# Branch products of two branches moved ahead of the gates in a one-core fp32 attention and feed-forward block

## The chip, the cores and the metric

The kernel runs on one core of a Trainium2 chip. The metric is device time in microseconds (us) of one execution; the median of three runs of the kernel before is 1457.66 us (1457.46 to 1459.04). A core has TensorE (PE: matmuls, and PEld for its weight loads), VectorE (DVE), ScalarE (ACT), GpSimd (POOL) and SyncE (SP, which here issues most of the DMAs). Each engine works through its own queue in order, and they wait for one another by semaphores.

## The reference, cut to what matters

One layer for 256 tokens of width 2048, all in fp32. The part that the change touches:

```python
h = rms_norm(x, g_mix[l]); proj = h @ w_in[l]
fq, fk, fv, f_logit, sq, sk, sv, mq, gates = jnp.split(proj, cuts, axis=-1)
o_fox = ...   # forgetting attention, 6 heads
o_sb  = ...   # stick-breaking attention, 6 heads
o_mem = ...   # attention to 256 memory tokens, 4 heads
g = jax.nn.sigmoid(gates.reshape(b, s, N_BRANCH, D_MODEL) + b_gate[l])
merged = (g[:, :, 0] * (o_fox @ w_br_fox[l])
          + g[:, :, 1] * (o_sb @ w_br_sb[l])
          + g[:, :, 2] * (o_mem @ w_br_mem[l]))
x = x + merged @ w_out[l]
```

Then a gated feed-forward part with a short causal convolution follows.

## The kernel before, in words

**Arithmetic.** Every fp32 weight piece (128 partitions x 1024 columns, `raw`) is split into a high part `hi` by a ScalarE copy and a low part `lo` by a VectorE subtraction (`piece`, L137 to L148, for plain products; `parts`, L374 to L380, in blocks). The pools hold four buffers each of `raw`, `hi` and `lo`. A product is then three matmuls (`three`, L382 to L386): high times high, low times high (both with `hi`), and high times `lo`; the third, L386, is the first that needs `lo`. The activations (`xT`, `oT`, `mT`) are the stationary side, 128 x 128; the weights stream with 512 columns.

**Plain products.** `product` (L158 to L173) runs over the k-tiles two at a time: one 512 KB load, one split, twelve matmuls into two PSUM banks (two row halves t), then one `tick`. `proj` is `product` with `xT` and `w_in`.

**Blocks.** `blocked` (L423 to L541) computes 1024 columns for all 16 k-tiles, in eight pairs of k-tiles, by a plan of letters. An "e" pair takes eight 2x2 block products, 24 matmuls. An "s" pair takes seven products after Strassen, 21 matmuls, from sums of weights and sums of activations. For gates the weight sums are formed on VectorE in `prepared` (L492 to L500, four 512-column additions), which is called at the end of the "e" pair before; the activation sums `xs` come from `x_sums` (L1041). The results X of the direct products hold four PSUM banks, the shared products Y four more, from the first "s" pair on. Just before that pair `ready` runs the queue of pending work dry and loads the gate's two bias tiles. After the last "s" pair `gathered` (L1104) adds the Ys up on VectorE, in steps beside the last two "e" pairs; after the block `scaled_sums` (L1132) adds X times the row scale, and a sigmoid on ScalarE finishes the gate (L1149 to L1151).

**Order.** Work that shall run beside matmuls is a generator, given to `later`. Each `tick` (L104) advances the generators that are active (at most `window` of them, two or three) by a step; a number yielded is a count of ticks to skip. `background` generators are advanced by ticks of plain products and of all blocks but the gates'. Two of them matter: `x_sums`, and `half_sums` (L264), which forms sums of weights of later stages: load, sums, store, with a period in ticks. `ready` and `finish` run ticks until nothing is pending. Instructions go to the engines' queues by a list scheduler that works from program order and its own estimate of when operands are there; those given to `in_order` keep their program order among themselves, and in the gate stage all matmuls of `three` do (`ordered`, L1093).

**The stage.** The six stick-breaking heads (`sb_head`, L988) are queued three at a time. Heads 3 to 5 end in the plain gate block that follows. For each half m of the 2048 columns the three gates come first (branch order 0 forget, 1 stick-breaking, 2 memory), then for two pieces n of 512 columns the three branch products (order: forget, memory, stick-breaking; L1154 to L1168), multiplied with the gates straight from PSUM and added up on VectorE; `merged_T` transposes the sum, and the product with `w_out` follows. By `g_plans` (L228) the first gate of the first half has the plan "", that is plain products of 16 k-tiles for each of its two pieces (L1138 to L1144); the other five have "esesesee", three "s" pairs out of eight. The sigmoids of the plain gate are queued by `sigmoids` (L1088) when the second gate's block reaches its first "s" pair. All these tiles (gates, sums of gate weights, heads) are of one pool of 14 buffers, 128 x 1024 (`block`).

Of the kernel before, what the change touches and what calls it, by code (L numbers as in the profile page):

```python
# [10 lines left out]
F32 = mybir.dt.float32  # L11
F32R = mybir.dt.float32r
AF = mybir.ActivationFunctionType
ALU = mybir.AluOpType
AX = mybir.AxisListType

P = 128
S = 256
NT = S // P
# [24 lines left out]
def hybrid_block(  # L44
# [25 lines left out]
    nc = tc.nc  # L70
# [26 lines left out]
    waiting, active, window = deque(), [], [2]  # L97

    def later(gen):
        waiting.append(gen)  # L100
# [18 lines left out]
    issued = set()  # L119
# [105 lines left out]


    o_plans = ("eessssse", "eessssse")
    g_plans = (("", "esesesee", "esesesee"), ("esesesee", "esesesee", "esesesee"))  # L228
    d_plans = (
        "efefefef" + "sef" * 4 + "ssefsfssfssee",  # L230
        "efsss" * 3 + "efssfsssssee",
# [4 lines left out]
    in_order = tc.keep_in_program_order  # L236
# [428 lines left out]
    gp = mix.enter_context(tc.tile_pool(name="gp", bufs=3))  # L665

    def block(name, dt=F32):
        return bp.tile([P, 1024], dt, tag="blk", name=name)
# [4 lines left out]
    def rows_of(b):  # L673
        return b.rearrange("p (t n) -> p t n", t=NT)
# [68 lines left out]
    w = {}  # L743
# [295 lines left out]
    xs = cst.tile([P, GS, 4, 2, P], F32R, tag="xres", name="xs")  # L1039

    def x_sums():  # L1041
        for _ in range(4):
            yield
        for p in range(GS):
            pair_sums(xT.pair(p), (junk(f"xa_{p}"), junk(f"xr_{p}")), [(xs[:, p], slice(0, 4))])
            for _ in range(3):
                yield

    background.append(x_sums())
    background.append(  # L1050
        half_sums(lambda name: gp.tile([P, 1024], F32, tag="pre", bufs=1, name=name), 8, 2, 5, "merged")
    )


# [30 lines left out]

    raw_g = lambda name: wp.tile([P, PIECE], F32, tag="raw", name=name)

    def sigmoids(tiles):  # L1088
        for v in tiles:
            in_order(nc.scalar.activation(v, v, AF.Sigmoid))  # L1090
            yield

    ordered[0] = True  # L1093
    for m in range(2):
        gate = []
        for b, plan in enumerate(g_plans[m]):
            g, bias = [], []

            def biases(m=m, b=b, bias=bias):
                for n in (2 * m, 2 * m + 1):  # L1100
                    bias.append(gp.tile([P, 512], F32, tag="bg", name=f"bg_{n}_{b}"))
                    nc.sync.dma_start(bias[-1], b_gate[0, b, n * 512 : (n + 1) * 512].partition_broadcast(P))

            def gathered(n0, Y, m=m, b=b, g=g, bias=bias):  # L1104

                w = block(f"gw_{m}_{b}")
                g += [rows_of(block(f"g_{m}_{b}_{n}")) for n in range(2)]
                e, f = w[:, :512], w[:, 512:]
                scaled = lambda dst, src, c, n: nc.vector.scalar_tensor_tensor(
                    dst, src, c, bias[n], ALU.mult, ALU.add  # L1110
                )
                nc.scalar.copy(e, Y[0])
                scaled(g[0][:, 0], Y[0], rstd[:, 0:1], 0)
                nc.vector.tensor_tensor(e, e, Y[1], ALU.add)
                yield
                nc.vector.tensor_tensor(f, e, Y[2], ALU.add)
                scaled(g[1][:, 0], f, rneg[:, 0:1], 1)
                nc.vector.tensor_tensor(f, e, Y[3], ALU.add)
                scaled(g[0][:, 1], f, rstd[:, 1:2], 0)
                yield  # L1120
                nc.vector.tensor_tensor(f, f, Y[2], ALU.add)
                scaled(g[1][:, 1], f, rneg[:, 1:2], 1)

            def ready():
                finish()
                if "heads" not in issued:
                    issued.add("heads")
                    window[0] = 2
                    later(sigmoids(gate[0] + gate[1]))
                biases()  # L1130

            def scaled_sums(n, ps, add):  # L1132
                for t in range(NT):
                    nc.vector.scalar_tensor_tensor(g[n][:, t], ps[t], rstd[:, t : t + 1], add[t], ALU.mult, ALU.add)

            c0 = C_GATE + b * D + m * PIECE
            gate.append(g)
            if not plan:  # L1138
                biases()
                for n in range(2):  # L1140
                    ps = proj(c0 + n * 512, 512, f"g{n}_{b}")
                    g.append(rows_of(block(f"g_{m}_{b}_{n}")))
                    scaled_sums(n, ps, [bias[n]] * NT)
                continue  # L1144
            X = blocked(
                "g", w_in, f"{m}{b}", c0, plan, lambda p, j: xT(2 * p + j), lambda p, f: xs[:, p, f], raw_g, block,
                gathered, ready,
            )
            for n in range(2):  # L1149
                scaled_sums(n, [X[t][n] for t in range(NT)], [g[n][:, t] for t in range(NT)])  # L1150
                nc.scalar.activation(g[n], g[n], AF.Sigmoid)  # L1151
        if m == 1:
            later(merged_sums())
        for n in range(2):  # L1154
            acc = gate[branches[0][3]][n]
            for i, (w, k0, nk, b) in enumerate(branches):
                ps = product(lambda k: oT[:, k0 + k], w[0], nk, (2 * m + n) * 512, 512, f"b{2 * m + n}_{b}")
                if (m, n, i) == (1, 0, 1):
                    xres = cst.tile([P, NT, D], F32, tag="xres", name="xres_again")
# [270 lines left out]
```

## Time and profile before

| | before |
|---|---|
| median of 3 runs | 1457.66 us |
| the profiled execution | 1457.28 us |
| its span, first to last instruction | 1455.6 us |
| granted TensorE clock | 1.000 |
| HBM read, written | 353.24 MB, 43.00 MB |

The rows of the profile name a line of the kernel (L386), an engine, an operation and its tiles, output<-inputs, with buffer numbers left out. In rows in order of time the first number is the start in us from the span's beginning, the second the length, and a bracket at the end tells how long the engine stood idle before the row and what released it. Matmul rows overlap: the time from one start to the next is what a matmul costs in a dense stream. The names: `raw_g`, `hi_g`, `lo_g` are weight pieces of a gate, `t_g`, `hi_t_g`, `lo_t_g` the sums of them, `xg` and `yg` the banks X and Y, `g` the gate tiles (and the banks of the plain gate), `gw` the scratch tile of `gathered`, `b` the banks of branch products, `z` and `sb` the bank and tile of a stick-breaking head, `fx` and `fa` those of a forget head, `pre_d` and `kept_d` the sums for a later stage.

### The profile page before, as it was taken

The numbers are of one execution on the slowest core, as the hardware profiler recorded it, in microseconds if no ns is written. First come the engines' busy times: TensorE is split into PE (matmuls) and PEld (weight loads), VectorE is DVE, ScalarE is ACT, GpSimd is POOL, SyncE is SP. The second block draws the span as 40 slices with busy tenths as digits, with TensorE's granted clock in tenths as the row PEclk, the third lists the DMA queues.
The fourth block names the chain that finished last, engine by engine and source line by source line (L and its number), as shares of the span: only waits on it lengthen the run. The fifth ranks groups of instructions, "written<-read, shape, count | busy, mean of one in ns | idle before, by whom it ended". The sixth has DMA issues, their size and how long they took to land.

```text
span 1455.6 us, 20647 instructions
## 1 busy us (share of the span) xinstructions
PE 1449.9 (100%) x7289; PEld 1226.9 (84%) x7289; DVE 1228.8 (84%) x1824; ACT 857.0 (59%) x1222; POOL 32.7 (2%) x70
## 2 busy tenths in 40 slices
PE   9999999999999999999999999999999999999998
PEld 7888888888888888888888888888888888888887
DVE  5788778776898899998887888888888877999988
ACT  6755445464564556546676656556556556676775
POOL 0000011010000000000000000000000011000000
PEclk9999999999999999999999999999999999999999
DMA  8797899777668576788877888888888899889996
GB/s 293 228 349 249 320 334 324 266 254 217 210 204 269 180 226 201 268 263 266 300 216 240 287 271 300 280 272 301 280 284 295 271 257 253 260 283 344 322 340 231
DMA packets 169414, 393.41 MB, mean 270 GB/s; under 512 B 12906, under 2 KB 30206, under 8 KB 165086
## 3 DMA queue, kind: packets, MB, share of 16 engines
q1 hardware_dynamic: 165822, 384.87, 79.5%
q0 software_dynamic: 2160, 5.12, 1.9%
q10 hardware_dynamic: 1328, 2.11, 0.4%
q8 instruction: 57, 0.93, 0.2%
q14 instruction: 47, 0.39, 0.1%
HBM read 353.24 MB, written 43.00 MB: 272 GB/s over the span
## 4 chain that ended last, share of the span: by engine, by line
PE 99%; DMA 0%; SPq 0%; DVE 0%; ACT 0%; issue 0%; DVEq 0%
PE u L1318 22%; PE u L1319 11%; PE xg L384 4%; PE xg L386 4%; PE xg L385 4%; PE xd L386 3%; PE xd L385 3%; PE xd L384 3%; PE s L386 2%; PE s L384 2%; PE f L384 2%; PE f L386 2%; PE f L385 2%; PE s L385 2%; PE b L386 2%; PE b L384 2%
## 5 line engine op out<-in xcount | busy, mean ns | idle before, releaser
L1318 PE MATMUL u<-hT,hi_u 128*128 128x512 f32 x1232 | 428.4, 394 | 0.0
L1319 PE MATMUL u<-hT,lo_u 128*128 128x256 f32 x1232 | 341.3, 277 | 0.0
L1318 PEld LDWEIGHTS u<-hT,hi_u 128*128 128x128 f32 x1232 | 231.0, 188 | 53.6
L144 DVE TENSOR_TENSOR lo_u<-raw_u,hi_u 128x1024 fp32r<-128x1024 f32 x176 | 215.2, 1223 | 72.0 <-ACT hi_u L143 71.7
L143 ACT CAST hi_u<-raw_u 128x1024 fp32r<-128x1024 f32 x176 | 184.7, 1050 | 134.7 <-PE u L1318 105.6
L1319 PEld LDWEIGHTS u<-hT,lo_u 128*128 128x128 f32 x1232 | 231.3, 188 | 0.0
L379 DVE TENSOR_TENSOR lo_d<-raw_d,hi_d 128x1024 fp32r<-128x1024 f32 x88 | 106.8, 1222 | 12.6 <-ACT hi_d L378 10.6
L378 ACT CAST hi_d<-raw_d 128x1024 fp32r<-128x1024 f32 x88 | 91.7, 1053 | 36.0 <-PE xd L385 14.2
L378 ACT CAST hi_g<-raw_g 128x1024 fp32r<-128x1024 f32 (+1 forms) x80 | 77.1, 972 | 47.1 <-PE xg L385 21.3
L379 DVE TENSOR_TENSOR lo_g<-raw_g,hi_g 128x1024 fp32r<-128x1024 f32 (+1 forms) x80 | 88.7, 1119 | 5.7 <-ACT hi_g L378 5.3
L386 PE MATMUL xg<-lo_g,xT 128*128 128x512 f32 x175 | 68.1, 389 | 0.0
L384 PE MATMUL xg<-hi_g,xT 128*128 128x512 f32 x175 | 68.1, 389 | 0.0
L385 PE MATMUL xg<-hi_g,xT 128*128 128x512 f32 x175 | 68.1, 389 | 0.0
L143 ACT CAST hi_f<-raw_f 128x1024 fp32r<-128x1024 f32 (+1 forms) x40 | 38.5, 967 | 47.8 <-PE f L385 27.6
L1318 PE MATMUL u<-hT_rest,hi_u 128*128 128x512 f32 x176 | 62.0, 394 | 0.0
L143 ACT CAST hi_b<-raw_b 128x1024 fp32r<-128x1024 f32 x32 | 33.7, 1052 | 45.5 <-PE b L385 18.5
L144 DVE TENSOR_TENSOR lo_f<-raw_f,hi_f 128x1024 fp32r<-128x1024 f32 (+1 forms) x40 | 44.4, 1117 | 18.4 <-ACT hi_f L143 18.4
L144 DVE TENSOR_TENSOR lo_s<-raw_s,hi_s 128x1024 fp32r<-128x1024 f32 (+1 forms) x40 | 44.6, 1123 | 17.8 <-ACT hi_s L143 17.8
L1268 ACT ACTIVATE y<-u,taps 128x256 f32<-128x256 f32 x88 | 49.5, 595 | 16.4 <-DVE u L1263 16.0
L143 ACT CAST hi_s<-raw_s 128x1024 fp32r<-128x1024 f32 (+1 forms) x40 | 38.3, 960 | 33.7 <-PE s L385 20.2
L378 ACT CAST hi_t_g<-t_g 128x1024 fp32r<-128x1024 f32 x30 | 31.5, 1051 | 42.0 <-PE xg L385 40.3
L378 ACT CAST hi_t_d<-raw_t_d 128x1024 fp32r<-128x1024 f32 (+1 forms) x54 | 43.5, 835 | 19.3 <-PE xd L385 11.9
(555 smaller groups left out, 3546.4 us busy)
## 6 DMA issues: line engine op xcount, KB each, us to landing
raw_u<-in_w_up_dram SPq DMA_DIRECT2D x176, 512.0 KB, 4.9
raw_g<-in_w_in_dram SPq DMA_DIRECT2D x96, 512.0 KB, 4.5
raw_d<-in_w_down_dram SPq DMA_DIRECT2D x61, 512.0 KB, 5.5
pre_d<-in_w_down_dram SPq DMA_DIRECT2D x17, 1024.0 KB, 7.4
kept_d<-pre_d SPq DMA_DIRECT2D x17, 1024.0 KB, 6.9
raw_f<-in_w_in_dram SPq DMA_DIRECT2D x32, 512.0 KB, 5.7
raw_s<-in_w_in_dram SPq DMA_DIRECT2D x32, 512.0 KB, 5.8
raw_t_d<-kept_d SPq DMA_DIRECT2D x27, 512.0 KB, 6.5
```

Source lines behind the costliest of these rows:

```text
L143: pin(nc.scalar.copy(hi[:, :m], raw[:, :m]))
L144: pin(nc.vector.tensor_tensor(lo[:, :m], raw[:, :m], hi[:, :m].bitcast(F32), ALU.subtract))
L378: nc.scalar.copy(hi[:, :n], src)
L379: nc.vector.tensor_tensor(lo[:, :n], src, hi[:, :n].bitcast(F32), ALU.subtract)
L384: fix(nc.tensor.matmul(o, lhsT=ah, rhs=w[0], start=first, stop=False))
L385: fix(nc.tensor.matmul(o, lhsT=al, rhs=w[0], start=False, stop=False))
L386: fix(nc.tensor.matmul(o, lhsT=ah, rhs=w[1], start=False, stop=last))
L1268: nc.scalar.activation(y, u[:, 2:], AF.Identity, scale=tap(2), bias=tap(3))
L1318: nc.tensor.matmul(ps[i], lhsT=hi[:, j, c], rhs=hT(k + j), start=first, stop=False)
L1319: nc.tensor.matmul(ps[i][:, :S], lhsT=lo[:, j, c], rhs=hT(k + j)[:, :S], start=False, stop=last)
```

## The change

Four products, those of the forget and the memory branch for the two pieces of the first half, are computed before the first gate, while the last heads are pending. Eight ScalarE copies put them into four tiles, `early`. The first half's gates then come in the order forget, memory, stick-breaking (0, 2, 1), all with the plan "esesesee". Behind the sigmoids of gate 0 each 1024-column piece is multiplied with its early product; behind those of gate 2 as well, and the result is added to gate 0's. In the product stage of the first half only the stick-breaking product is left. `sigmoids` goes away, `ready` sets the window to two each time. `x_sums` starts three ticks earlier, and `half_sums` has a period of 6 in place of 8 and stores after 4 ticks, not 5. The second half is as it was.

```diff
-    g_plans = (("", "esesesee", "esesesee"), ("esesesee", "esesesee", "esesesee"))
+    g_plans = (("esesesee", "esesesee", "esesesee"), ("esesesee", "esesesee", "esesesee"))
...
     def x_sums():
-        for _ in range(4):
-            yield
+        yield
...
-        half_sums(lambda name: gp.tile([P, 1024], F32, tag="pre", bufs=1, name=name), 8, 2, 5, "merged")
+        half_sums(lambda name: gp.tile([P, 1024], F32, tag="pre", bufs=1, name=name), 6, 2, 4, "merged")
...
-    def sigmoids(tiles):
-        for v in tiles:
-            in_order(nc.scalar.activation(v, v, AF.Sigmoid))
-            yield
-
     ordered[0] = True
+    early = {}
+    for w, k0, nk, b in branches[:2]:
+        for n in range(2):
+            ps = product(lambda k: oT[:, k0 + k], w[0], nk, n * 512, 512, f"b{n}_{b}")
+            early[n, b] = rows_of(block(f"early_{n}_{b}"))
+            for t in range(NT):
+                nc.scalar.copy(early[n, b][:, t], ps[t])
     for m in range(2):
-        gate = []
-        for b, plan in enumerate(g_plans[m]):
+        gate = {}
+        order = [b for *_, b in branches] if m == 0 else range(3)
+        for b in order:
+            plan = g_plans[m][b]
...
             def ready():
                 finish()
-                if "heads" not in issued:
-                    issued.add("heads")
-                    window[0] = 2
-                    later(sigmoids(gate[0] + gate[1]))
+                window[0] = 2
                 biases()
...
-            gate.append(g)
-            if not plan:
-                biases()
-                for n in range(2):
-                    ps = proj(c0 + n * 512, 512, f"g{n}_{b}")
-                    g.append(rows_of(block(f"g_{m}_{b}_{n}")))
-                    scaled_sums(n, ps, [bias[n]] * NT)
-                continue
+            gate[b] = g
...
             for n in range(2):
                 scaled_sums(n, [X[t][n] for t in range(NT)], [g[n][:, t] for t in range(NT)])
                 nc.scalar.activation(g[n], g[n], AF.Sigmoid)
+                if m == 0 and (n, b) in early:
+                    nc.vector.tensor_tensor(g[n], g[n], early[n, b], ALU.mult)
+                    if b:
+                        nc.vector.tensor_tensor(gate[0][n], gate[0][n], g[n], ALU.add)
...
         for n in range(2):
             acc = gate[branches[0][3]][n]
             for i, (w, k0, nk, b) in enumerate(branches):
+                if m == 0 and (n, b) in early:
+                    continue
                 ps = product(lambda k: oT[:, k0 + k], w[0], nk, (2 * m + n) * 512, 512, f"b{2 * m + n}_{b}")
```

## The prediction

> **What bounds the kernel now.** I read the page first (its first part, then the chain that ended last), then the busy times by stage, then the rows of TensorE, VectorE and ScalarE in time order around the gate blocks.
>
> ```profile
> span 1455.6 us, 20647 instructions
> PE 1449.9 (100%) x7289; PEld 1226.9 (84%) x7289; DVE 1228.8 (84%) x1824; ACT 857.0 (59%) x1222; POOL 32.7 (2%) x70
> PE 99%; DMA 0%; SPq 0%; DVE 0%; ACT 0%; issue 0%; DVEq 0%
> ```
>
> The chain is TensorE from end to end. A busy TensorE alone proves little, since matmuls overlap, so I look at start times. These are the first and the last of 24 consecutive matmuls of an eight-product pair:
>
> ```profile
> 359.95 0.39 PE L384 MATMUL xg<-hi_g,xT 128*128 128x512 f32 x1
> ...
> 365.16 0.39 PE L386 MATMUL xg<-lo_g,xT 128*128 128x512 f32 x1
> ```
>
> 23 steps in 5.21 us: a 512-column matmul costs 0.2266 us of stream although each row shows 0.39. The gate block's window below has 185 in 41.50 us, 0.224 each, so it holds no gap that could be removed: in this stage time changes only through the number of matmuls, or through a stall that is not there yet. [...]
>
> The stages: rest of the heads with ten steps of the plain block, the last six plain steps, the gate block of branch 1, that of branch 2.
>
> ```profile
> 308.60:344.00 35.40, 35.40 (x172) 30.10 (x172) 29.99 (x47) 23.21 (x38) 3.81 (x12) 1.00 0.91 296
> 344.00:360.00 16.00, 16.00 (x72) 13.21 (x72) 7.76 (x10) 5.07 (x7) 0.00 (x0) 1.00 0.59 174
> 360.00:401.50 41.50, 41.50 (x185) 34.37 (x184) 37.08 (x45) 24.87 (x27) 0.00 (x0) 1.00 0.68 210
> 401.50:443.00 41.50, 41.50 (x185) 34.37 (x184) 37.45 (x45) 24.23 (x26) 0.00 (x0) 1.00 0.69 218
> ```
>
> Columns: length, then busy time and count of TensorE, its weight loads, VectorE, ScalarE, GpSimd, then clock, DMA share, GB/s. In a gate block with sevens VectorE is busy 37.1 to 37.5 of 41.5 us: about 4 us from being the bound. In the plain block's tail it is busy 7.8 of 16. The change removes the plain block and gives a third block of the dense kind.
>
> **Term 1, matmuls.** The plain block has 16 k-tiles x 2 row halves x 2 column halves x 3 = 192. With "esesesee" it has five pairs of 24 and three of 21, so 183. The branch products are moved, not altered. 9 x 0.2266 = 2.04 us less on the path.
>
> **The early products.** Do their operands exist, and do the last heads still find cover?
>
> ```profile
> L837 PE MATMUL fa<-fx,vf x12: 377/377/378, 214.0 to 263.4; 128*128 128x256 f32 x12
> L837 PE MATMUL z<-sb,vs x12: 377/379/382, 311.4 to 343.2; 128*128 128x256 f32 x12
> ```
>
> The last forget head leaves at 263.4, 45 us before the first early product; memory heads were queued ahead of it. Stick-breaking heads 3 to 5 start at the second step after 308.6 and by their yields (2, 1, 2) issue their last matmuls at the tenth. The early products give 3+3+2+2 = 10 steps of the same 12 matmuls, and the first pair of the next block two more before the first seven drains the queue. The covers match; price 0. If a head slipped, up to those two steps' 5.4 us are its margin.
>
> ScalarE gets eight copies out of PSUM; the nearest row is a copy of the same shape:
>
> ```profile
> L1112 ACT COPY gw<-yg x5: 576/577/580, 387.7 to 599.0; 128x512 f32<-128x512 f32 x5
> ```
>
> 8 x 0.577 = 4.6 us onto 23.21 busy of 35.40 makes 79%; hidden under TensorE, price 0, at most one copy (0.6) per change of product if banks run short. VectorE loses the plain block's two scaled sums there and gains one half's sums. The x-sums' earlier start costs nothing: the same instructions, in a stretch with 5.4 us free on VectorE.
>
> Queues: SyncE gets the ten 512 KB branch loads ahead of the gate loads, the same number and size per step as the plain block's; block 0's two bias loads move behind the first pair. The half-pair sums keep their number by my count of steps (48 steps at period 8, then 32 at period 6 plus what the w_out stage still runs: six halves in both), but the last one's sums now fall into the first steps of w_out. They are 0.7+0.4+0.4 us for VectorE, which at that place has
>
> ```profile
> 663.33 2.48 DVE L379 TENSOR_TENSOR lo_o<-raw_o,hi_o 128x1024 fp32r<-128x1024 f32 x2 [2.31 <-ACT hi_o L378]
> ```
>
> 2.31 us idle. Price 0, or 1.5 without that cover.
>
> **Term 2, the multiplies between gate blocks.** This is where I expect the loss. Today the gates of the first half are multiplied with PSUM in the product stage, behind plain products. Now, right after the sigmoids of block 0, VectorE gets two 1024-column multiplies, and after block 2 two multiplies and two additions. The same shape from SBUF, and the pitch of two such in a row (below, 409.16: 2.35 for two, so 1.13 each):
>
> ```profile
> L254 DVE TENSOR_TENSOR pre_d<-pre_d x23: 680/1218/1220, 315.1 to 1155.3; 128x1024 f32<-128x1024 f32 x17, 128x512 f32<-128x512 f32 x6
> ```
>
> So 2 x 1.13 = 2.27 us at the first boundary and 4.53 us at the second. What margin is there at such a boundary? Today's boundary from branch 1 to 2, VectorE:
>
> ```profile
> 386.89 1.23 DVE L379 TENSOR_TENSOR lo_t_g<-t_g,hi_t_g 128x1024 fp32r<-128x1024 f32 x1 [1.43 <-ACT hi_t_g L378]
> ...
> 399.45 0.68 DVE L1121 TENSOR_TENSOR gw<-gw,yg 128x512 f32<-128x512 f32 x1
> 400.05 0.75 DVE L1134 SCALAR_TENSOR_TENSOR g<-xg,scales,g 128x512 f32<-128x512 f32 x1
> 400.71 0.74 DVE L1109 SCALAR_TENSOR_TENSOR g<-gw,scales,bg 128x512 f32<-128x512 f32 x1
> 401.37 2.07 DVE L1134 SCALAR_TENSOR_TENSOR g<-xg,scales,g 128x512 f32<-128x512 f32 x3
> 403.35 0.68 DVE L497 TENSOR_TENSOR t_g<-raw_g,raw_g 128x512 f32<-128x512 f32 x1
> 403.95 0.69 DVE L498 TENSOR_TENSOR t_g<-t_g,raw_g 128x512 f32<-128x512 f32 x1
> 404.56 0.69 DVE L379 TENSOR_TENSOR lo_g<-raw_g,hi_g 128x512 fp32r<-128x512 f32 x1
> 405.16 0.69 DVE L499 TENSOR_TENSOR t_g<-t_g,raw_g 128x512 f32<-128x512 f32 x1
> 405.76 1.22 DVE L379 TENSOR_TENSOR lo_g<-raw_g,hi_g 128x1024 fp32r<-128x1024 f32 x1
> 406.89 2.35 DVE L379 TENSOR_TENSOR lo_t_g<-t_g,hi_t_g 128x1024 fp32r<-128x1024 f32 x2
> 409.16 2.35 DVE L379 TENSOR_TENSOR lo_g<-raw_g,hi_g 128x1024 fp32r<-128x1024 f32 x2
> ...
> 418.17 1.23 DVE L379 TENSOR_TENSOR lo_t_g<-t_g,hi_t_g 128x1024 fp32r<-128x1024 f32 x1 [1.37 <-ACT hi_t_g L378]
> ```
>
> Between 386.89 and 418.17 no row has an idle bracket. The low part made at 405.76 is ready at 406.98; its reader is
>
> ```profile
> 408.00 0.39 PE L386 MATMUL xg<-lo_g,xT 128*128 128x512 f32 x1
> ```
>
> a lead of 1.02 us. Whatever is put into VectorE's queue before 405.76 beyond that stops TensorE. Would the multiplies stand there? ScalarE at the same time:
>
> ```profile
> 398.68 0.62 ACT L378 CAST hi_g<-raw_g 128x512 fp32r<-128x512 f32 x1 [1.67 <-PE xg L385]
> 401.40 1.05 ACT L378 CAST hi_g<-raw_g 128x1024 fp32r<-128x1024 f32 x1 [2.10 <-PE xg L385]
> 402.36 2.23 ACT L1151 ACTIVATE g<-g 128x1024 f32<-128x1024 f32 x2
> 404.50 1.03 ACT L378 CAST hi_t_g<-t_g 128x1024 fp32r<-128x1024 f32 x1
> ```
>
> The 512-wide high part is there at 399.30, yet its low part starts at 404.56, behind eight instructions that are earlier in the program and became ready later. So earlier in the program goes first. The sigmoids end near 403.4 and 404.6, before 405.76; the multiplies are program-earlier than all splits of the next block and land ahead of the critical one. Lateness: 2.27 - 1.02 = 1.25 us at the boundary 0 to 2, and 4.53 - 1.02 = 3.51 us at the boundary 2 to 1. Bounds: 3.0 for the second if the additions slip behind the critical split and its two successors (each read six matmuls, 1.36 us, after the one before, but 1.13 apart on VectorE, so the leads there are 1.25 and 1.48, and 4.53 - 1.48 = 3.0); 0 for both if all slip to the idle brackets such as 418.17, which the queue order speaks against. Nothing here can be below zero: no lead grows. After each boundary the brackets of 1.4 us restore the lead, and what waits behind a late split is only TensorE.
>
> What is saved in exchange, twelve 512-column operations in the product stage, such as
>
> ```profile
> L1168 DVE TENSOR_TENSOR g<-g,g x16: 682/684/689, 457.8 to 659.2; 128x512 f32<-128x512 f32 x16
> ```
>
> is no time, since TensorE does not wait there.
>
> **Term 3, the table.** The first sigmoid moves to the boundary 0 to 2 and brings its table load along:
>
> ```profile
> 359.92 1.06 ACT L378 CAST hi_g<-raw_g 128x1024 fp32r<-128x1024 f32 x1 [2.10 <-PE g L385]
> 361.00 1.28 ACT L1090 ACT_TABLE_LOAD   x1
> 362.29 1.06 ACT L1090 ACTIVATE g<-g 128x1024 f32<-128x1024 f32 x1
> ```
>
> Both sigmoids then end 1.28 later, near 404.7 and 405.9, and VectorE, in order, may stand before the first multiply: 0.8 us if only the instruction at 403.35 is ahead of it, 0 if the three up to 404.56 are. I take 0.4, the middle. [...]
>
> **Sum.** -2.04 + 1.25 + 3.51 + 0.4 = +3.1 us. The profiled execution took 1457.28 us, span 1455.6 and 1.7 around it, 0.4 below the median of 1457.66; on the median the forecast is 1460.8 us, slower by 0.21%. A measurement of this kernel can tell about 0.2% (2.9 us) from no change, so this lies on that edge. The case's own range, with terms 2 and 3 at their ends (second boundary 3.0 to 3.5, table 0 to 0.8), is +2.2 to +3.6, and a little semaphore time per stall: 1459.8 to 1461.6.
>
> **Rivals.** *The multiplies hide.* If they are queued behind the critical splits, or VectorE enters the boundary with more lead, only term 1 is left: 1457.66 - 2.04 = 1455.6 us, not slower. For it: the brackets of 1.4 us per third of a block could hold 4 us of work. Against it: the order at 399.45 to 405.76. It decides at a lead of 4.5 us instead of 1.02.
>
> *The branch weights land late as well.* The first plain steps stand in the stage with DMA share 0.91, and
>
> ```profile
> raw_g<-in_w_in_dram SPq DMA_DIRECT2D x96, 512.0 KB, 4.5
> raw_b<-in_w_br_fox_dram SPq DMA_DIRECT2D x12, 512.0 KB, 5.1
> ```
>
> a branch piece lands 0.6 us later than a gate piece. If the first two early pieces come that much late and no lead is there, it adds 1.2: +4.3, 1462.0 us. Against it: the chain that ended last has 0% of DMA today, with the same loads in it.
>
> [...]
>
> That the change does not do what it says I rule out: plan, products and multiplies are all in the diff.
>
> **Chances.** Forecast case 0.62, a little over half of it above 2.9 us; multiplies hide 0.22; late weights 0.09; drain 0.03; 0.04 for a gain over 0.2%, for which I see no mechanism, as 2.04 us is all that is removed. Slower by over 0.2%: 0.34 + 0.09 + 0.03 = 0.46; within: 0.28 + 0.22 = 0.50; faster: 0.04. The range reaches from the hidden case with a little noise, 1455.3, to the late weights, 1462.2.
>
> **What would show it.** Right: nine matmuls fewer; three equal gate blocks with sevens in the first half; a TensorE gap of 1 to 2 us at the first seven of branch 2's block and of 3 to 4 us at that of branch 1's, released by the low-part splits, with multiplies ahead of them on VectorE. Wrong: multiplies standing after those splits, or starts 0.227 apart throughout; gaps in the early products; a stall at the first seven of block 0, where heads would have slipped.

## The result, and the profile after

| | before | after |
|---|---|---|
| median, runs of one comparison | 1457.71 us (1456.89 to 1459.04, 6 runs) | 1464.04 us (1462.58 to 1465.87, 6 runs) |
| the profiled execution | 1457.28 us | 1464.39 us |
| its span | 1455.6 us | 1462.7 us |

The ratio is 1.0043 with a 95% interval of 1.0032 to 1.0053: slower by 6.3 us. A second comparison of the same two kernels (`e0_again` below) gave 1.0052 [1.0035, 1.0070], by the medians 1.0047. The ratios take in all runs, and a few much slower ones (one of e0_again at 1476.91 us, one of e8 at 1470.69, six of the 23 of the kernel before beside e8 and e9 at 1466.4 to 1469.9) move them, so there the medians are the better guide. Forecast were 1460.8 us and a range from 1455.3 to 1462.2: the sign was right, the loss is twice as large, and the time lies beyond the range.

From the page after: the span, the busy times, and the chain that ended last.

```profile
span 1462.7 us, 20671 instructions
PE 1452.4 (99%) x7280; PEld 1227.7 (84%) x7280; DVE 1245.5 (85%) x1844; ACT 864.8 (59%) x1237; POOL 32.4 (2%) x70
PE 98%; DVE 1%; ACT 0%; DMA 0%; issue 0%; SPq 0%; DVEq 0%
```

There are nine matmuls fewer, as forecast, and VectorE is in the chain now. Busy times by stage, in the columns of the prediction: rest of the heads with the early products, then the gate blocks of branch 0, 2 and 1.

```profile
310.40:345.30 34.90, 34.90 (x169) 29.43 (x168) 30.52 (x49) 26.05 (x45) 4.23 (x12) 1.00 0.81 267
345.30:386.90 41.60, 41.60 (x187) 34.45 (x186) 34.88 (x42) 21.46 (x25) 0.00 (x0) 1.00 0.63 196
386.90:430.20 43.30, 42.12 (x185) 34.26 (x184) 40.96 (x50) 25.14 (x27) 0.00 (x0) 1.00 0.66 207
430.20:477.00 46.80, 43.57 (x184) 35.27 (x183) 41.44 (x48) 24.22 (x25) 0.00 (x0) 0.96 0.63 200
```

The first block runs through. The second takes 1.7 us more for the same 185 matmuls, the third 5.3 us more, and there the clock column drops to 0.96: not in the forecast.

Where the time went, by the starts of the first matmul of each stage in the two profiles:

| stage | before | after | difference |
|---|---|---|---|
| start to the last heads' projections done | 308.66 | 310.32 | +1.7 |
| from there to the output product (`w_out`) | 348.56 | 353.81 | +5.25 |
| output product | 83.03 | 83.28 | +0.25 |
| the rest | 715.3 | 715.3 | 0 |

The first row is not the change's doing: the first stick-breaking projection, ahead of all that the change touches, already starts 1.7 us later (193.0 before, 194.75 after). In the other fourteen profiles it starts between 192.9 and 194.3, at 193.8 in that of the changed kernel run again. The second row holds the loss. TensorE at the boundary from branch 2 to 1, in order of time:

```profile
435.80 0.39 PE L385 MATMUL yg<-hi_g,xT 128*128 128x512 f32 x1
439.24 0.50 PE L386 MATMUL yg<-lo_g,xT 128*128 128x512 f32 x1 [3.05 <-DVE lo_g L379]
...
440.38 0.51 PE L386 MATMUL xg<-lo_g,xT 128*128 128x512 f32 x1 [0.17 <-DVE lo_g L379]
440.72 0.60 PE L384 MATMUL xg<-hi_g,xs 128*128 128x512 f32 x1
...
444.11 0.43 PE L386 MATMUL yg<-lo_t_g,xs 128*128 128x512 f32 x1
444.37 0.39 PE L384 MATMUL xg<-hi_t_g,xT 128*128 128x512 f32 x1
```

The gap is the forecast one, released by the low-part split: 3.44 us from 435.80 to 439.24 in place of 0.227, and with the smaller ones up to 440.72 it makes 3.78 us. What follows is new. From 440.72 to 444.37 nine steps take 3.65 us, 0.41 each, where nine normal ones take 2.04: 1.61 us more, with no wait in any row. The trace's clock records show why: 0.5 from 440.74 on, for 3413 ns. VectorE ahead of the gap:

```profile
432.15 1.23 DVE L1146 TENSOR_TENSOR g<-g,early 128x1024 f32<-128x1024 f32 x1
433.30 0.68 DVE L497 TENSOR_TENSOR t_g<-raw_g,raw_g 128x512 f32<-128x512 f32 x1
433.90 1.22 DVE L1148 TENSOR_TENSOR g<-g,g 128x1024 f32<-128x1024 f32 x1
435.04 1.21 DVE L1146 TENSOR_TENSOR g<-g,early 128x1024 f32<-128x1024 f32 x1
436.17 0.68 DVE L498 TENSOR_TENSOR t_g<-t_g,raw_g 128x512 f32<-128x512 f32 x1
436.77 1.21 DVE L1148 TENSOR_TENSOR g<-g,g 128x1024 f32<-128x1024 f32 x1
437.91 0.68 DVE L499 TENSOR_TENSOR t_g<-t_g,raw_g 128x512 f32<-128x512 f32 x1
438.51 1.82 DVE L379 TENSOR_TENSOR lo_g<-raw_g,hi_g 128x512 fp32r<-128x512 f32 x2
```

Two multiplies (L1146) and two additions (L1148) stand ahead of the low part at 438.51 for which TensorE waits, as argued from the boundary before. One detail differs: the prediction took its lead at the 1024-wide split, but TensorE stops first at the 512-wide one just ahead of it, which had 2.07 us of lead before (ready at 405.25, read at 407.32). The last sum of `t_g` (L499), which stood behind that split before, now stands ahead of it as well. At the boundary from branch 0 to 2 the same picture is smaller: the gaps from 392.56 on add up to 1.73 us, and the clock stays at 1.00. So −2.04 + 1.73 + 3.78 + 1.61 = +5.1 of the 5.25 us are accounted for.

### The profile page after: what moved, and what is told of

Its sections match the earlier page's. It is cut to its first block, busy times and chain, and to the rows that moved or that the text cites. A ratio compares the mean times of both kernels' runs of the same rounds, so it can differ in the third digit from the quotient of the medians.

```text
span 1462.7 us, 20671 instructions
## 1 busy us (share of the span) xinstructions
PE 1452.4 (99%) x7280; PEld 1227.7 (84%) x7280; DVE 1245.5 (85%) x1844; ACT 864.8 (59%) x1237; POOL 32.4 (2%) x70
## 4 chain that ended last, share of the span: by engine, by line
PE 98%; DVE 1%; ACT 0%; DMA 0%; issue 0%; SPq 0%; DVEq 0%
PE u L1317 22%; PE u L1318 11%; PE xg L386 4%; PE xg L384 4%; PE xg L385 4%; PE xd L385 3%; PE xd L384 3%; PE xd L386 3%; PE s L386 2%; PE s L384 2%; PE f L384 2%; PE f L386 2%; PE s L385 2%; PE f L385 2%; PE b L386 2%; PE b L384 2%
## 5 line engine op out<-in xcount | busy, mean ns | idle before, releaser
L378 ACT CAST hi_g<-raw_g 128x1024 fp32r<-128x1024 f32 (+1 forms) x96 | 92.7, 973 | 55.8 <-PE xg L385 28.4
L379 DVE TENSOR_TENSOR lo_g<-raw_g,hi_g 128x1024 fp32r<-128x1024 f32 (+1 forms) x96 | 106.0, 1117 | 3.9 <-ACT hi_g L378 3.3
L386 PE MATMUL xg<-lo_g,xT 128*128 128x512 f32 x210 | 82.0, 390 | 0.3 <-DVE lo_g L379 0.3
L384 PE MATMUL xg<-hi_g,xT 128*128 128x512 f32 x210 | 82.0, 390 | 0.0
L385 PE MATMUL xg<-hi_g,xT 128*128 128x512 f32 x210 | 81.7, 389 | 0.0
L378 ACT CAST hi_t_g<-t_g 128x1024 fp32r<-128x1024 f32 x36 | 37.9, 1052 | 53.5 <-PE xg L385 44.4
L379 DVE TENSOR_TENSOR lo_t_g<-t_g,hi_t_g 128x1024 fp32r<-128x1024 f32 x36 | 43.6, 1220 | 19.5 <-ACT hi_t_g L378 19.5
L384 PE MATMUL s<-hi_s,xT 128*128 128x512 f32 (+1 forms) x140 | 54.2, 387 | 0.0
```

What stands on the lines that cost most here:

```text
L378: nc.scalar.copy(hi[:, :n], src)
L379: nc.vector.tensor_tensor(lo[:, :n], src, hi[:, :n].bitcast(F32), ALU.subtract)
L384: fix(nc.tensor.matmul(o, lhsT=ah, rhs=w[0], start=first, stop=False))
L385: fix(nc.tensor.matmul(o, lhsT=al, rhs=w[0], start=False, stop=False))
L386: fix(nc.tensor.matmul(o, lhsT=ah, rhs=w[1], start=False, stop=last))
```

## The experiments

Theory, after the result: the VectorE work at the boundaries makes the two gaps, and the longer gap costs the halved clock besides. Rival: something that came with it (the table load, the reordered gates, a chance of the clock). A second question came up on the way: the output product lost between 0.1 and 3.3 us in some kernels and nothing in others. "Before" below is the kernel before in the same comparison.

| kernel | median us | before | ratio [95%] | first 140 matmuls of the output product, us |
|---|---|---|---|---|
| before | | | | 32.70 |
| after | 1464.04 | 1457.71 | 1.0043 [1.0032, 1.0053] | 32.80 |
| e0_again | 1464.69 | 1457.87 | 1.0052 [1.0035, 1.0070] | 33.30 |
| e1_mult_mid_block | 1457.94 | 1457.87 | 0.9998 [0.9989, 1.0006] | 34.59 |
| e2_adds_late | 1460.70 | 1457.87 | 1.0020 [1.0011, 1.0029] | 32.85 |
| e3_table_early | 1463.73 | 1457.87 | 1.0040 [1.0027, 1.0053] | 33.78 |
| e4_long_first_gap | 1464.57 | 1457.95 | 1.0047 [1.0034, 1.0061] | 33.25 |
| e5_sums_before_w_out | 1456.96 | 1457.95 | 0.9993 [0.9984, 1.0002] | 32.70 |
| e6_before_late_sums | 1457.46 | 1457.95 | 1.0000 [0.9991, 1.0009] | 32.70 |
| e7_one_addition | 1463.57 (one run) | 1457.95 | | 35.02 |
| e8_before_sums_shifted | 1462.09 | 1458.41 | 1.0020 [1.0001, 1.0038] | 35.85 |
| e9_sums_spread | 1456.29 | 1458.41 | 0.9973 [0.9956, 0.9990] | 32.70 |
| e10_other_buffer | 1459.29 | 1457.53 | 1.0013 [1.0004, 1.0021] | 32.70 |
| e11_after_other_buffer | 1465.45 | 1457.53 | 1.0054 [1.0041, 1.0068] | 32.70 |
| e12_one_buffer | 1456.04 | 1457.64 | 0.9990 [0.9982, 0.9999] | 33.21 |
| e13_after_one_buffer | 1463.63 | 1457.64 | 1.0042 [1.0028, 1.0055] | 34.34 |

### The boundaries: e0 to e4, e7

**e0_again** is the changed kernel once more.

> The changed kernel once more, to see what of its 6.3 us is steady. Theory A (VectorE's multiplies ahead of the splits, then the halved clock): gaps of 1.7 and 3.8 us at the two first sevens again, clock 0.5 for about 3.4 us after the second, 5.0 us over before from these. Theory C (a part of the loss, 1.74 us in the profiled execution, is from the start of the kernel and is chance): the first branch product starts anywhere between 308.6 and 310.4 us, and with the earlier start the time is about 1462.5 instead of 1464. If the later start belongs to the program, it is 310.3 again.

Gaps of the same size at both boundaries, and again 3413 ns at half clock behind the second. The first branch product starts at 309.79, half a microsecond earlier than after, but the median is not lower: the late start in the profile of after does not carry the loss.

**e1_mult_mid_block** takes multiplies and additions away from the boundary: a generator, started by `ready` of the next block, issues the multiplies in mid-block, and the additions go to the product stage.

```diff
+    def multiplied(g, b):
+        yield 2
+        for n in range(2):
+            nc.vector.tensor_tensor(g[n], g[n], early[n, b], ALU.mult)
+            yield 3
...
+                while pend:
+                    later(pend.pop())
...
-                if m == 0 and (n, b) in early:
-                    nc.vector.tensor_tensor(g[n], g[n], early[n, b], ALU.mult)
-                    if b:
-                        nc.vector.tensor_tensor(gate[0][n], gate[0][n], g[n], ALU.add)
+            if m == 0 and (0, b) in early:
+                pend.append(multiplied(g, b))
```

> The four multiplies move into the middle of the next gate block (from its sixth and tenth step), the two additions into the product stage; all else as in the changed kernel. Theory A: no gap at the first sevens, clock 1.0 throughout, only the nine matmuls fewer are left: 2.0 us under before, about 1455.7. Theory B (the third dense block or the sigmoids on ScalarE make the gap, not the multiplies): gaps of 1 us and more stay at both first sevens, and the time stays above 1460.

Its three gate blocks, and VectorE at its boundary from branch 0 to 2:

```profile
343.80:385.40 41.60, 41.60 (x187) 34.56 (x187) 34.71 (x42) 22.48 (x27) 0.00 (x0) 1.00 0.62 193
385.40:427.00 41.60, 41.60 (x185) 34.48 (x184) 40.85 (x49) 25.07 (x26) 0.00 (x0) 1.00 0.71 217
427.00:468.50 41.50, 41.50 (x184) 34.37 (x183) 40.26 (x48) 24.22 (x25) 0.00 (x0) 1.00 0.71 218
```

```profile
390.78 1.22 DVE L379 TENSOR_TENSOR lo_g<-raw_g,hi_g 128x1024 fp32r<-128x1024 f32 x1
391.91 2.36 DVE L379 TENSOR_TENSOR lo_t_g<-t_g,hi_t_g 128x1024 fp32r<-128x1024 f32 x2
394.18 2.36 DVE L379 TENSOR_TENSOR lo_g<-raw_g,hi_g 128x1024 fp32r<-128x1024 f32 x2
396.45 1.23 DVE L1094 TENSOR_TENSOR g<-g,early 128x1024 f32<-128x1024 f32 x1
```

The multiply now stands at 396.45, behind five splits. VectorE is as busy as after (40.85 us in the second block, 40.96 after) and there is no gap and no halved clock: the place made the loss, not the amount of work in the block (the two additions now run in the product stage). The stretch up to the output product takes 346.51 us, 2.05 less than before: term 1 of the prediction by itself. Yet the kernel only ties with the kernel before, since its output product took 84.97 us in place of 83.0.

**e2_adds_late** leaves the multiplies at the boundary and moves only the two additions into the product stage; **e7_one_addition** leaves one of them there too.

```diff
-                    if b:
-                        nc.vector.tensor_tensor(gate[0][n], gate[0][n], g[n], ALU.add)
...
-        if m == 1:
-            later(merged_sums())
+        later(merged_sums() if m else added(gate[0], gate[2]))
```

> Only the two additions move, to the product stage; the multiplies stay behind the sigmoids at both boundaries. Theory A: the first gap stays 1.7 us, the second falls from 3.8 to 1.3 to 1.6 us (2.27 - 1.02 plus the passing on), the clock stays 1.0: +1.0 to 1.3 us over before, about 1459. If the clock fell for a reason other than the length of the gap, it falls here too and costs another 1.6. Theory B: the second gap stays above 3.

> Multiplies at both boundaries, one of the two additions at the second, the other in the product stage. Theory A: the second gap lies between those of none (1.3) and two additions (3.8), at 2.6 us. The clock stays 1.0 if a gap must last about 3.2 us to halve it; if it drops to 0.5 after this gap too, the limit is lower.

First boundary of e2 as after, 1.74 us; second 1.51 in place of 3.78, and the clock stays. It takes 4.0 us less than e0_again, its neighbour in the same comparison; by the gaps it should be 2.27 + 1.61 = 3.9. Its total was missed all the same: 1.0 to 1.3 us over before were expected, the span of its profile is 1.8 longer than that of before (0.5 of it a gap at the first branch product) and the median 2.8 above. What the other executions lost besides, no trace shows. With one addition (e7) the idle comes in two pieces of 1.5 and 0.9 us, both shorter than the 3.2 us of after, and the clock halves all the same. The windows view of e7 and then of e2, each for the 3.41 us ahead of 437.9 and the 3.41 us behind:

```profile
434.48:437.89 3.41, 1.37 (x5) 0.85 (x6) 3.41 (x6) 1.49 (x2) 0.00 (x0) 1.00 0.34 94
437.93:441.34 3.41, 3.41 (x10) 2.63 (x9) 3.41 (x4) 1.52 (x2) 0.00 (x0) 0.50 0.61 208
```

```profile
434.48:437.89 3.41, 2.45 (x10) 1.51 (x9) 3.41 (x5) 2.16 (x3) 0.00 (x0) 1.00 0.52 154
437.93:441.34 3.41, 3.41 (x16) 2.81 (x15) 3.41 (x4) 1.48 (x2) 0.00 (x0) 1.00 0.69 175
```

TensorE busy for 1.37 us of such a stretch was followed by clock 0.50 and ten matmuls in the next, 2.45 by clock 1.00 and sixteen. (The stretches are steps of e7's clock, whose grid the last section describes; in e2's own step, 435.95 to 439.36, TensorE was busy for 2.68.)

**e3_table_early** loads the sigmoid's table behind the last head, by a sigmoid of two columns.

```diff
+                if "heads" not in issued:
+                    issued.add("heads")
+                    warm = sm.tile([P, 16], F32, tag="nwa", name="warm")
+                    nc.scalar.activation(warm[:, :2], oT[:, N_FOX + N_SB - 1, :2].bitcast(F32), AF.Sigmoid)
```

> A sigmoid of 128x2 elements behind the last head's output loads the table before the first gate block's sevens; its result is not used. Theory A with the table as a part of the first gap: the bracket of 0.23 us before the first multiply goes and the first gap falls from 1.7 to about 1.5; the second stays 3.8: 0.2 us faster than the changed kernel, not visible in its time. Theory B (ScalarE's late sigmoids make the first gap): the first gap falls by the load's 1.28, to 0.4.

The first boundary's gaps shrink from 1.73 to 1.50 us: the table cost 0.23. In this profile the clock was halved for 6827 ns, two windows in a row, so the time shows none of it.

**e4_long_first_gap** is e2 with two more multiplies, into tiles that nothing reads, at the first boundary.

```diff
+                    if b == 0:
+                        in_order(nc.vector.tensor_tensor(block(f"more_{n}"), early[n, b].rearrange("p t n -> p (t n)"), early[n, b].rearrange("p t n -> p (t n)"), ALU.mult))
```

> As the run with the additions late, but two multiplies more (128x1024, results unused) at the first boundary, so that the first gap is made as long as the second was. Theory A (the length of the gap halves the clock, wherever it stands): first gap 1.7 + 2.3 = 4.0 us, then the clock at 0.5 for one window of 3.4 us (1.6 us lost) or two (3.2), now at the first boundary; second gap 1.3 to 1.6 with the clock at 1.0: 3.9 to 5.5 us over the run with the additions late. If the drop belonged to the second boundary itself, the clock stays 1.0: 2.3 over.

The long gap is now at the first boundary (3.0 and 0.75 us at 393.3 and 396.9), and so is the halved clock, from 397.5 on; the second boundary has 1.5 us and full clock. The rival falls: the halved clock goes where the idle time goes, with table, order of gates and sums unchanged.

### The output product: e5, e6, e8 to e13

**e5_sums_before_w_out** is e1 with the half sums at a period of 5 and at most six of them; **e6_before_late_sums** is the kernel before with a period of 9 and the store after 4, which pushes its sixth half into the output product.

> The multiplies in mid-block and, besides, the six half-pair sums with a period of 5 and at most six, so that the last one's load and store (0.5 MB each) are issued before the w_out stage as in the kernel before. Theory D (what the mid-block run lost again in the w_out stage, 84.97 us instead of 83.03, is the last half's transfers competing with that stage's loads): the w_out stage takes 83.0 again, and the time is 2.0 us under before, 1455.8. If the w_out stage varies by itself, it stays between 83.1 and 85.0.

> The kernel before with one thing changed: half-pair sums with period 9 (store after 4 ticks), so that the sixth half is loaded one tick before the w_out stage and stored in it. Theory D: the w_out stage grows from 83.0 to between 83.3 and 85, and the time by 0.3 to 2 us, with no gap in the gate stage. If the transfers do not matter: 83.0 and the time of before.

e5 has 83.00 us there, and 1456.96 us; 1455.8 was expected. Of the difference, 0.8 us were lost ahead of the output product (347.30 us in place of the 346.51 of e1), most of it in one gap at 653.5, where a branch product waits for VectorE. But e6 has 83.00 as well, though its last store is issued only 0.4 us ahead of the first output-product matmul (1.7 us behind it in e1): a miss, which said that lateness alone was not it.

**e8_before_sums_shifted** starts the half sums of the kernel before six ticks later, storing after 4.

> The kernel before with the timing of the half sums alone changed: the generator waits six ticks first and stores after four, so that the load of the sixth half is issued one tick ahead of the output product's start, its sums fall one tick into that product and its store three ticks in, as in the changed kernel. In the profiles so far the time from the first output-product matmul to the first matmul of u was 83.0 us where the sums were done by then, and 83.2 to 85.3 in the seven kernels that had the changed kernel's timing. Theory 1, the late half-sum transfers are the cause: this length grows to 83.2 to 85.3 here, with gaps at the second or third pair of the output product, and the kernel takes 0.2 to 2.3 us more than the kernel before (1458 to 1460 us). Theory 2, they are not, and something else of the changed kernels (which tiles are free, the order of the loads) is: 83.0, and the time is that of the kernel before.

86.27 us, the largest loss so far, in a kernel that has nothing else of the change. (It lost 1.8 us before the output product besides, at a branch weight that landed late.) So the half sums' timing does it, but not in e6. The difference is in SyncE's queue. SyncE in e1, at the output product's start (656.5):

```profile
658.17 0.53 SPq L283 DMA_DIRECT2D kept_d<-pre_d  x1
660.51 3.86 SPq L475 DMA_DIRECT2D raw_t_o<-kept_o  x2
664.46 0.42 SPq L471 DMA_DIRECT2D raw_o<-in_w_out_dram  x1
664.93 0.42 SPq L472 DMA_DIRECT2D raw_o<-kept_o  x1
665.46 0.37 SPq L440 DMA_DIRECT2D raw_o<-in_w_out_dram  x1
```

and the longest wait of SyncE there, in its view of waits:

```profile
SPq L475 <- DMA kept_d<-pre_d: 3.1, 1, 3.1
```

The row at 660.51 holds two loads. The second, weight sums of k-pair 3 (the fourth "s" pair; the expectations below call it the third seven), takes its buffer in turn from six places, one of which is the staging tile `pre` of the half sums (`raw_tile`, L1191, and L1201 of the changed kernel). It must wait until the half sum's store has landed, 3.1 us, and the loads of the next pair, due earlier, stand behind it in SyncE's queue. ScalarE, which casts these pieces, in e1:

```profile
671.97 1.05 ACT L378 CAST hi_o<-raw_o 128x1024 fp32r<-128x1024 f32 x1 [2.87 <-DMA raw_o<-kept_o]
673.48 1.04 ACT L378 CAST hi_o<-raw_o 128x1024 fp32r<-128x1024 f32 x1 [0.45 <-DMA raw_o<-in_w_out_dram]
674.76 1.57 ACT L378 CAST hi_t_o<-raw_t_o 128x1024 fp32r<-128x1024 f32 x2 [0.24 <-DMA raw_t_o<-kept_o]
```

and the same pieces in e9, where no store is under way:

```profile
669.36 1.05 ACT L387 CAST hi_o<-raw_o 128x1024 fp32r<-128x1024 f32 x1 [0.57 <-PE yo L394]
670.75 1.06 ACT L387 CAST hi_o<-raw_o 128x1024 fp32r<-128x1024 f32 x1 [0.33 <-PE xo L394]
672.11 1.57 ACT L387 CAST hi_t_o<-raw_t_o 128x1024 fp32r<-128x1024 f32 x2 [0.30 <-PE yo L394]
```

In e1 the casts wait for transfers, in e9 for TensorE to free their output, as they should. In e6 that load stands behind the next pair's loads, and waits for no store.

**e9_sums_spread** is e1 with the six halves at fixed ticks: early products, middles of gate blocks, branch products of the first half.

```diff
-    background.append(
-        half_sums(lambda name: gp.tile([P, 1024], F32, tag="pre", bufs=1, name=name), 6, 2, 4, "merged")
+    always.append(
+        half_sums(
+            lambda name: gp.tile([P, 1024], F32, tag="pre", bufs=1, name=name),
+            ((0, 2, 5), (11, 17, 20), (59, 61, 63), (65, 71, 74), (81, 87, 90), (97, 103, 106)),
+        )
```

> The kernel with the multiplies in mid-block, and the six half sums spread: loads in the early products, in the middles of gate blocks and in the branch products of the first half, none in those of the second half nor in the output product. Theory 1 (the output product lost its time to late half sums, and nothing else is lost): no gap at the gate blocks' boundaries, 83.0 us from the first output-product matmul to the first of u, and the 2.04 us of the nine matmuls removed come through: 1455.6 to 1456.0 us, ratio 0.9986. Theory 2 (VectorE has no room left in gate blocks for 1.5 us of sums beside the multiplies): gaps of 0.5 to 2 us at low parts in the blocks that got sums, and 1457 to 1459 us. Rival to both: the output product's loss comes without late sums too: 83.2 to 85.3 us there and about 1457 us.

No gap in the three blocks, 83.00 us in the output product, 1456.29 us: faster than both kernels. By the medians it is 2.1 us below the kernel before, a ratio of 0.9985; the 0.9973 of the table overstates it. Its span, 1454.5 us, is 1.1 below that of before; with the start at the same point (193.0 there, 193.5 here) it would be 1.6.

**e10_other_buffer** (on e1) and **e11_after_other_buffer** (on the changed kernel) give the output product's loads a tile of the block pool in place of `pre`. Sums, transfers and their order stay, but for the load that waited.

```diff
-    raw_o = lambda name: raw_tile(name, lambda name: gp.tile([P, PIECE], F32, tag="pre", bufs=1, name=name))
+    raw_o = lambda name: raw_tile(name, block)
```

> The kernel with the multiplies in mid-block, its late sixth half sum left where it was (load before the output product, sums and store in it); only the weight loads of the output product that took the half sums' staging buffer in turn now take one of the block pool. With that, the load of the third seven's weight sums no longer stands in SyncE's queue behind a store that has to land: it stood there 3.1 us, ahead of the loads of the next pair, in the profile with the multiplies in mid-block. Theory A, that wait in SyncE's queue is the loss: 83.0 us from the first output-product matmul to the first of u, no gap there, and 1455.7 to 1456.3 us. Theory B, the half sum's own transfers and VectorE additions are the loss: they are unchanged, so 83.7 to 85.3 us with gaps at 670 to 690, and about 1458 us as with the multiplies in mid-block alone.

> The changed kernel with the same one edit: the output product's loads take a buffer of the block pool in place of the half sums' staging buffer. Its gate block boundaries are as in the changed kernel, so 1.7 and 3.8 us of gaps and a halved clock for 3.4 us stay. Theory A, the wait in SyncE's queue is what the output product lost: 83.0 us from its first matmul to the first of u, and 0.2 to 2 us less than the changed kernel, 1462.5 to 1463.8 us. Theory B, late transfers and additions: 83.2 to 85.3 us as before and 1464 us.

By the total, both missed: 87.25 and 85.89 us in the output product. By the place, they answer. The first 140 matmuls take 32.70 us, as without late sums, where e1 took 34.59: additions and transfers cost nothing there. The loss is a new one, at the second 1024 columns:

```profile
697.77 0.50 PE L386 MATMUL xo<-lo_o,mT 128*128 128x512 f32 x1 [0.54 <-DVE lo_o L379]
700.11 0.65 PE L384 MATMUL xo<-hi_o,mT 128*128 128x512 f32 x1 [1.12 <-DVE e L417]
```

Ahead of them ScalarE starts no cast from 690.09 to 695.41. By the trace's semaphores the load that its next cast needs was issued at 687.32 and landed at 695.31. Why it came so late was not tested; SyncE's longest wait there (3.4 us, for a tile of VectorE's gathering) ends only at 703.7, behind both gaps, and is not their cause. With the halved clock behind these gaps the new loss costs 4.2 us in e10.

**e12_one_buffer** (on e1) and **e13_after_one_buffer** (on the changed kernel) therefore change the buffer of that one load alone.

```diff
+    raw_o = lambda name: raw_tile(name, block if name.startswith("raw_t_o0") else staged)
```

> The kernel with the multiplies in mid-block, and of the output product's loads only the one that stood behind the half-sum store (the weight sums of its third seven in the first 1024 columns) takes a buffer of the block pool; the second 1024 columns take the staging buffer as in the changed kernel. The late half sum stays. Theory A, the wait in SyncE's queue is all that the output product loses in this kernel: 32.70 us for its first 140 matmuls, as with the buffer changed everywhere, no gap at the second 1024 columns, 83.0 us to the first matmul of u, and 1455.8 to 1456.4 us. Theory B, the half sum's transfers and additions cost something of their own later on: more than 83.2 us with gaps behind the 140th matmul, and 1457 us or more.

> The changed kernel with the same edit of one load. The boundary gaps and the halved clock stay: 353.5 to 353.8 us from the last head's projections to the output product. Theory A: 83.0 us in the output product, and 0.3 to 0.7 us less than the changed kernel's profiles showed there, so 1463.3 to 1464.3 us. Theory B: 83.2 us or more there, 1464 to 1465 us.

The output product took 83.53 and 84.73 us, so theory A, which asked for 83.0, missed in both. The times, 1456.04 and 1463.63 us, lie where A put them, and the loss of e12 stands in the first 140 matmuls and not behind them, where B put it: neither theory holds as stated. `pre` then goes to the first load of the second 1024 columns, which takes the same place in SyncE's queue and waits for the same store (2.9 and 3.5 us). e12 is still faster than before, 0.9990 [0.9982, 0.9999].

Over all profiles: SyncE waits 2.9 to 4.0 us for that store in ten kernels (after, e0 to e4, e7, e8, e12, e13), and in all ten the first 140 matmuls take 32.80 to 35.85 us. In the six without it (before, e5, e6, e9, e10, e11; 0.2 us at most) they take 32.70, also in e10 and e11, whose late sums are those of e1 and of the changed kernel. That it is this wait is shown for these 140 matmuls; why one and the same code lost 0.25 us in one profile and 0.66 in the next stays open.

## Why the prediction was right or wrong

**Term 1** (−2.04) was right: 7280 matmuls, and −2.05 us in e1, where nothing else moves.

**The early products at price 0** were right: from the end of the last heads' projections to the first eight-product pair it took 51.29 us before and takes 34.98 after, 16.31 less, which are the 72 matmuls by which the early products are fewer than the plain block (72 x 0.2266 = 16.3). The late branch weights, a rival there, showed in e4: ScalarE waits 1.29 us for one, and TensorE loses 0.54 us. In e0, e2 and e3 TensorE loses 0.3 to 0.5 us at the same place, but there the weight had landed 0.7 to 0.9 us before its cast began, which stood behind a cast of the x sums (`xs`, L400) that waited 1.5 us for VectorE. So `x_sums`, whose earlier start the prediction called free, had a part in these gaps, though no run moves it alone; in the profile of after the place cost 0.1 us.

**Term 2, the mechanism,** was right: the multiplies land ahead of the critical split, the lead is about 1 us, and TensorE waits. Its first gap with the table's part was forecast as 1.25 + 0.4 = 1.65 and measured 1.73, the second as 3.51 and measured 3.78. **Term 3** was 0.23 (e3) in place of 0.4, inside its bounds. So the multiplies alone cost 1.50 in place of 1.25, and that the first gap came out so close is luck: two misses of 0.2 cancel. The chances give 0.03 to a drain, idle time of ScalarE around the table load. No run shows one; the rows at the first sigmoid, in the profile of after, leave no room for it:

```profile
386.87 1.05 ACT L378 CAST hi_g<-raw_g 128x1024 fp32r<-128x1024 f32 x1 [1.97 <-PE xg L385]
387.94 1.28 ACT L1144 ACT_TABLE_LOAD   x1
389.23 2.01 ACT L1144 ACTIVATE g<-g 128x1024 f32<-128x1024 f32 x2
```

The cast ends at 387.92 and the load begins at 387.94; it ends at 389.22 and the sigmoid begins at 389.23.

**The step that failed** is the price of term 2's second gap. The prediction said "what waits behind a late split is only TensorE", and charged the idle time alone. Behind the idle time the granted clock was 0.5 for 3413 ns besides: +1.61 us, so that this boundary cost 5.4 us, not 3.5. No rival and no bound of the prediction had that term.

**The second failure** is "Price 0" for the half sums' last sums in the output product. It looked at VectorE's 2.31 us of idle time, which did cover them, and not at the staging tile's next user and at what stands behind that in SyncE's queue: +0.25 us in the profile of after, 0.7 and 1.1 in those of e0 and e3.

The sum of the parts is −2.04 + 1.73 + 3.78 + 1.61 + 0.25 = +5.3. By the medians it is 6.3 with an interval of 4.7 to 7.7, so parts and median agree within it, and the microsecond between them stays open; the profile's own 7.1 holds the 1.7 us of its late start. The rival *multiplies hide* was wrong for this kernel and became true by moving them: e9 came out at 1456.29 us, where the rival gave 1455.6.

## What to carry to other kernels

Where every engine's queue is in order and the bound engine's operands are ready only a microsecond ahead (1.02 us at the boundary in the kernel before), it matters where added work stands, not whether the engine has room: the same multiplies and additions cost 7 us at the blocks' boundaries, with the clock, and nothing with the multiplies five splits later and the additions in the product stage. A stall of TensorE is priced with the clock that follows it, not only with its length: behind the 3.78 us of gaps in after the clock was 0.5 for 3413 ns and cost 1.61 us more, behind the 1.51 us in e2 it stayed at 1.00. When a transfer's timing is moved, look up who takes its buffer next, and what is queued behind that load.

## What the runs showed of the hardware

**The clock halved behind short idle times, in windows of 3.4133 us.** In eight profiles (after, e0, e3, e4, e7, e10, e11, e13) the granted clock fell to 0.5 in mid-kernel, for 3413 ns or twice that, and always a whole number of steps of 3.4133 us (115 to 203 of them, within 0.01 us) after the clock's first release at the kernel's start. In after the release is at 10.661 us, where the step from matmul to matmul goes from 0.43 to 0.23 us; the fall comes 430.079 us behind it (126 steps), the end of the halved stretch 433.492 us (127) and the fall at the kernel's end 1450.664 us (425). In before the release is at 5.096 us, and the fall at the end comes 1450.664 us behind it as well. Such a step is called a window here. In the windows below the clock went with TensorE's busy time in the window just ended. The windows view of after, of e10, and of e8:

```profile
437.29:440.70 3.41, 1.28 (x4) 0.78 (x5) 3.41 (x5) 2.00 (x2) 0.00 (x0) 1.00 0.19 26
440.74:444.15 3.41, 3.41 (x10) 2.63 (x9) 3.41 (x4) 1.04 (x1) 0.00 (x0) 0.50 0.77 267
```

```profile
696.81:700.22 3.41, 1.75 (x7) 0.79 (x6) 3.41 (x5) 2.49 (x3) 0.00 (x0) 1.00 0.48 174
700.29:703.70 3.41, 3.41 (x9) 2.64 (x10) 3.41 (x7) 1.04 (x1) 0.00 (x0) 0.50 0.58 192
```

```profile
674.37:677.78 3.41, 2.21 (x10) 1.43 (x9) 0.78 (x3) 1.04 (x1) 0.00 (x0) 1.00 0.98 346
677.79:681.20 3.41, 2.83 (x12) 1.77 (x11) 3.12 (x5) 2.96 (x4) 0.00 (x0) 1.00 0.72 265
```

Busy for 1.28 or 1.75 us of the window, the next ran at 0.50; busy for 2.21, it did not, nor for 1.97 in another window of e8 (from 653.96). At half clock such figures do not carry over, since each matmul lasts longer (0.63 us a row in place of 0.39): in e3 and e13 a halved window in which TensorE was busy for 2.48 and 2.32 us, with six matmuls, was followed by a second halved one. e8 had more idle time than e10 in some 3.4 us (2.3 us from 676.0 on), but it fell into two windows; in e10, by the starts of the matmuls, 2.1 us of idle time lay in one window, most of it in two pieces of 0.7 and 1.3 us. So in these runs whether a gap of 2 to 3 us cost the clock depended on where the windows lay, and that moved from run to run: 3413 ns in after, 6827 in e3 and e13, for the same gap of 3.2 us, whose end there fell about 1 us into the halved window. At half clock the step from matmul to matmul was 0.427 us in place of 0.227 (after, 441.12 to 443.68).
